# Fourteen Strassen-like pairs in place of thirteen in the down projection of a hybrid decoder layer, with small tiles shared to make room

## The chip, the core and the metric

The kernel runs on one core of a Trainium2 chip. The metric is the device time of one execution in microseconds (us). The engines named below are TensorE (PE, the matrix engine; PEld is its loading of weights), VectorE (DVE), ScalarE (ACT), GpSimd (POOL) and SyncE (SP), whose queue issues nearly all DMA transfers. SBUF is the on-chip memory of 128 partitions from which the engines work, and PSUM holds the matmuls' sums in eight banks.

## The reference

One decoder layer for 256 tokens of width 2048, all in float32:

```
h   = RMSNorm(x);  proj = h @ W_in            (2048 x 6144)
A: 8 heads of stick-breaking attention         (no softmax, strictly causal)
B: 8 heads of rotary, dilated sliding-window attention
mix = concat(head-normalised A, B) @ W_out     (2048 x 2048)
x   = x + RMSNorm(mix)
u   = RMSNorm(x) @ W_up                        (2048 x 11008)
u   = causal depthwise convolution of width 3 over tokens, plus a bias
y   = gelu(gate half of u) * (value half of u) (256 x 5504)
x   = x + RMSNorm(y @ W_down)                  (5504 x 2048)
```

The result has to keep float32 accuracy.

## The kernel before

**Accuracy.** TensorE multiplies in a reduced float32 form. Each weight tile and each activation is therefore split in two: `high` (L86) rounds the tile on ACT into `wh`, `low` (L91) subtracts that from the tile on DVE and leaves the rest in `wl`. Each product is then three matmuls: high by high, activation's low by weight's high, activation's high by weight's low. In the down projection these are lines 597, 598 and 599 (`multiply`). Weights come in half-chunks of 128 x 1024 (512 KB) into five `raw` buffers; `wh` and `wl` have four buffers each.

**Stages.** A list of chunks of 1 MB runs through the value, query and key projections (L729 to L735, with the heads' attention stepped in between), the output projection, a hand-written and pinned passage for the two norms (L754 to L849), and then the 86 chunks of up (43 feature tiles, gate and value half). The chunk loop loads two chunks ahead and splits one ahead. After the loop the down projection runs on its own.

**Who sets the order.** The kernel is written for a framework that plans the order of each engine's instructions from the program order and its own durations, allocates tiles, and adds every wait. `pin` and `keep_in_program_order` bind an instruction to the written order.

**The up stage.** `convolved` (L463) handles one finished chunk. `both` (L125) copies one half of the PSUM sum into a tile `half` on ACT (L128) and adds the other half on DVE into `u` (L130). Then DVE multiplies by the norm's row `r2B` (L468), ACT applies the first tap and the bias into `cv` (L470), and DVE adds the other two taps from `u` (L471, L472). For the gate half ACT applies the gelu (L474). For the value half DVE multiplies gate and value, and stores the result for down: a feature tile that is a "single" goes to `yt` (L480 to L482), one that belongs to a pair goes into the tile `pair` (L487).

**Pairs and singles.** Two feature tiles that form a pair go through a fast 2 x 2 block product: the two k tiles, the two token tiles and the two column blocks of 512 need seven products in place of eight. When a pair's second tile is ready, DVE forms four sums of its blocks (L490 to L493), and ACT and DVE split all seven blocks (L494, L495) into `yp`. Of the 43 feature tiles, 13 pairs take 26 and 17 are singles. The weights' sums are formed in two steps. T13 is formed early: `presum` (L540) loads the two parts during attention and the output projection, adds them (L551) and stores the tile back to memory. Two more sums, T24, are formed in down by L580 and L582 in a part of `room`, the memory of the activations of up. A pair is then four units of work (Rb, Ra, T13 and T24, with 2, 1, 2 and 2 products, L504), a single is one unit of four products (L510).

**The down stage.** It runs twice, for the two halves (`cp`) of the output columns. `_down_plan` (L40) gives the order of pairs and singles: with `cp` 0 two singles first, then the pairs with 11 singles spread among them, then four singles; with `cp` 1 the pairs with 13 singles spread among them, and the last four singles held. `run` (L621) prepares units three ahead (`prepare`, L567: loads, `high`, `low`, T24's sums) and multiplies unit by unit. After the last pair `combine` (L602) adds the shared products with one copy on ACT (L606) and four additions on DVE (L607 to L610). After the first half, `close` (L612) adds each of four banks to the result (L617), takes the sum of squares (L412), and leaves a multiplication by the gain row `gbc` (L619) for later. The held singles go bank by bank, so that each bank can be closed while PE works on the next; the last is split in two halves of 256 columns. The row `gbc` is loaded into `room` and multiplied by -0.5 (L876) just before `down.run()`.

**Small tiles.** `ones` and `diag` serve `along_rows` (L281), which turns a per-token factor into a row by a matmul (L287). It is used by the first norm and, in the passage before up, by the second norm (L436). `phB` is the pool of up and down and takes the space of the attention's pool `apool` once that is closed (L850).

## Time and profile before

| | |
|---|---|
| median of 3 runs | 1117.37 us (1117.27 to 1118.07) |
| profiled execution | 1117.53 us, its span 1115.6 us |
| granted TensorE clock | 0.998 |
| busy: PE, PEld | 1103.6 us, 941.2 us |
| busy: DVE, ACT, POOL | 880.8 us, 658.6 us, 3.3 us |
| DMA moved | 257.79 MB, mean 231 GB/s |

Busy time is the time in which an engine works on instructions. Matmuls overlap, so that PE's busy time says little on its own: the step from one start to the next does. A row of the timeline has the start in us, the length in us, the engine, the line of the kernel, the operation, what it writes and reads, its shape and how many like it are merged; a bracket gives the idle time before it and what ended it. A grouped row has the count after the x, then busy us and the mean ns of one, then the engine's idle time before them. A row of waits gives us in total, how many times, and the longest.

### The profile page before, as it was taken

Reading aid. Unit: us, or ns where it says so; the run is one execution under the profiler, and the core shown is the slowest. Engines: PE = TensorE matmul, PEld = TensorE weight load, DVE = VectorE, ACT = ScalarE, POOL = GpSimd, SP = SyncE. Lnnn points to the kernel's source line nnn. Section 1 sums busy time; section 2 is a strip of 40 time slices with the busy share of each in tenths; the row PEclk is TensorE's granted clock in tenths of the full one; section 3 lists DMA queues with packets and bytes.
Section 4 is the critical chain, followed back from the end, with each engine's and each line's share of the span. In section 5 each row is a group of like instructions: output and inputs, shape, how many; then the busy total and the mean of one; then the engine's idle time right before and its main releaser. Section 6 shows DMA issues by size and latency. Waiting matters only on the chain.

```text
span 1115.6 us, 16292 instructions
## 1 busy us (share of the span) xinstructions
PE 1103.6 (99%) x5855; PEld 941.2 (84%) x5855; DVE 880.8 (79%) x1370; ACT 658.6 (59%) x1038; POOL 3.3 (0%) x10
## 2 busy tenths in 40 slices
PE   9999999999999999999999999999999999999996
PEld 6888888888888888888888888888888888888885
DVE  6577776777776589878888878888878898889887
ACT  6656655655654476655555555555555566666564
POOL 0000000000000000000000000000000000000000
PEclk9999999999999999999999999999999999999999
DMA  9977777878879856555555555555555577767775
GB/s 348 327 259 276 254 249 271 299 256 274 272 259 321 273 199 212 191 188 189 187 190 181 189 187 186 188 187 189 189 188 189 172 251 245 248 218 252 242 242 207
DMA packets 74817, 257.79 MB, mean 231 GB/s; under 512 B 8432, under 2 KB 9328, under 8 KB 73968
## 3 DMA queue, kind: packets, MB, share of 16 engines
q1 hardware_dynamic: 74448, 256.68, 69.0%
q8 instruction: 46, 0.75, 0.3%
q14 instruction: 35, 0.29, 0.1%
q10 hardware_dynamic: 288, 0.07, 0.0%
HBM read 238.89 MB, written 17.83 MB: 230 GB/s over the span
## 4 chain that ended last, share of the span: by engine, by line
PE 98%; DMA 1%; DVE 0%; ACT 0%; issue 0%; SPq 0%; DVEq 0%; ACTq 0%
PE mmu L101 28%; PE mmu L104 14%; PE mmqk L101 11%; PE p L598 7%; PE p L597 7%; PE p L599 6%; PE mmqk L104 5%; PE mmv L147 3%; PE mmo L143 3%; PE mmo L144 3%; PE mmo L147 3%; PE mmv L143 3%; PE mmv L144 3%; PE mmu L110 1%; DMA raw<-in_w_v 1%; PE po L317 0%
## 5 line engine op out<-in xcount | busy, mean ns | idle before, releaser
L88 ACT CAST wh<-raw 128x1024 fp32r<-128x1024 f32 (+1 forms) x413 | 419.5, 1023 | 362.7 <-PE mmu L101 189.6
L93 DVE TENSOR_TENSOR wl<-raw,wh 128x1024 fp32r<-128x1024 f32 (+1 forms) x413 | 487.7, 1187 | 170.8 <-ACT wh L88 167.3
L101 PE MATMUL mmu<-hT,wh 128*128 128x512 f32 x1344 | 340.9, 396 | 0.0
L101 PEld LDWEIGHTS mmu<-hT,wh 128*128 128x128 f32 x1344 | 240.2, 188 | 45.6
L104 PEld LDWEIGHTS mmu<-hT,wl 128*128 128x128 f32 x1344 | 182.9, 189 | 15.2
L104 PE MATMUL mmu<-hT,wl 128*128 128x256 f32 x1344 | 186.4, 281 | 0.0
L101 PE MATMUL mmqk<-hT,wh 128*128 128x512 f32 x512 | 133.0, 401 | 0.0
L101 PEld LDWEIGHTS mmqk<-hT,wh 128*128 128x128 f32 x512 | 92.0, 188 | 17.2
L104 PEld LDWEIGHTS mmqk<-hT,wl 128*128 128x128 f32 x512 | 69.9, 188 | 5.8
L598 PE MATMUL p<-wh,yp 128*128 128x512 f32 x182 | 71.7, 394 | 0.0
L597 PE MATMUL p<-wh,yp 128*128 128x512 f32 x182 | 71.3, 392 | 0.0
L104 PE MATMUL mmqk<-hT,wl 128*128 128x256 f32 x512 | 71.1, 281 | 0.0
L599 PE MATMUL p<-wl,yp 128*128 128x512 f32 x182 | 70.8, 389 | 0.0
L598 PE MATMUL p<-wh,yt 128*128 128x512 f32 (+1 forms) x140 | 54.2, 387 | 0.0
L597 PE MATMUL p<-wh,yt 128*128 128x512 f32 (+1 forms) x140 | 54.0, 385 | 0.0
L599 PE MATMUL p<-wl,yt 128*128 128x512 f32 (+1 forms) x140 | 53.3, 382 | 0.0
L470 ACT ACTIVATE cv<-u,par 128x256 f32<-128x256 f32 x86 | 51.5, 599 | 2.4 <-DVE u L468 2.3
L143 PE MATMUL mmv<-wh,hT 128*128 128x512 f32 x128 | 51.5, 403 | 0.7 <-ACT hT L225 0.6
L144 PE MATMUL mmv<-wh,hT 128*128 128x512 f32 x128 | 50.5, 395 | 0.3 <-DVE hT L248 0.3
L143 PE MATMUL mmo<-wh,mix 128*128 128x512 f32 x128 | 50.4, 394 | 0.0
L88 ACT CAST wh<-room 128x1024 fp32r<-128x1024 f32 x26 | 27.3, 1050 | 38.2 <-PE p L598 37.3
L144 PE MATMUL mmo<-wh,mix 128*128 128x512 f32 x128 | 49.9, 390 | 0.0
(173 smaller groups left out, 1207.2 us busy)
## 6 DMA issues: line engine op xcount, KB each, us to landing
raw<-in_w_up SPq DMA_DIRECT2D x172, 512.0 KB, 4.4
raw<-in_w_qk SPq DMA_DIRECT2D x64, 512.0 KB, 4.9
raw<-in_w_dn SPq DMA_DIRECT2D x60, 512.0 KB, 4.4
raw<-in_w_o SPq DMA_DIRECT2D x32, 512.0 KB, 4.8
raw<-in_w_v SPq DMA_DIRECT2D x31, 512.0 KB, 5.3
t<-in_w_dn SPq DMA_DIRECT2D x26, 512.0 KB, 5.7
t_kept<-t SPq DMA_DIRECT2D x26, 512.0 KB, 3.9
raw<-t_kept SPq DMA_DIRECT2D x26, 512.0 KB, 4.4
```

What stands on the lines that cost most here:

```text
L88: pin(A.copy(wh, raw))
L93: pin(V.tensor_tensor(wl, raw, wh.bitcast(F32), op=ALU.subtract))
L101: T.matmul(ps, wh[:, j * P:(j + 1) * P], h[:, k, :, :], start=(k == 0), stop=False, skip_group_check=True)
L104: T.matmul(ps[:, 0, :], wl[:, j * P:(j + 1) * P], h[:, k, 0, :], start=False, stop=(k == KT - 1), skip_group_check=True)
L110: T.matmul(ps[:, part, :], parts[k // 8][low][:, k % 8 * P:(k % 8 + 1) * P], h[:, k, part, :], skip_group_check=True, **kw)
L143: T.matmul(ps[t], hi[:, k, tc_], ws, start=(first and i == 0 and j == 0), stop=False)
L144: T.matmul(ps[t], lo[:, k, tc_], ws, start=False, stop=False)
L147: T.matmul(ps[t], hi[:, k, tc_], wl[:, j * 512:(j + 1) * 512], start=False, stop=(last and i == len(parts) - 1 and j == n - 1))
L470: A.activation(cv, u, AF.Identity, scale=cw(2), bias=par[:, P_CB + f:P_CB + f + 1])
L597: T.matmul(ps, yh, wh[:, cs], start=key not in self.begun, stop=False)
L598: T.matmul(ps, yl, wh[:, cs], start=False, stop=False)
L599: T.matmul(ps, yh, wl[:, cs], start=False, stop=self.left[key] == 0)
```

## The change

- There are 14 pairs and 15 singles. Pairs are still the tiles 3m and 3m+1.
- The first half of down opens with three singles. The others are spread with the count rounded up, so that a single comes after the first pair rather than later. Without the four at the end it is 8 singles among 14 pairs in the first half and 11 in the second.
- `presum` has 28 sums over 52 steps in place of 26 over every second step. An addition follows its load by two steps (before: three), a store by three (before: four).
- `both` copies into `u` itself and adds in place; `half` goes there. The value half's `cv` lies in the tile `pair`, the gate half's in a tile `gate`.
- `ones` and `diag` are one tile, allocated anew for the second norm under the tag `pair` and filled by GpSimd there.
- The multiplication of `gbc` by -0.5 comes in the middle of the first half of down.

```diff
-NPAIR = 13
+NPAIR = 14
+SUM_STEPS = 52
@@ _down_plan
-    plan = [("one", left.pop(0)) for _ in range(0 if cp else 2)]
+    plan = [("one", left.pop(0)) for _ in range(0 if cp else 3)]
...
-        plan += [("one", left.pop(0)) for _ in range((m + 1) * spread // NPAIR - m * spread // NPAIR)]
+        plan += [("one", left.pop(0)) for _ in range(-(-(m + 1) * spread // NPAIR) + (-m * spread // NPAIR))]
@@ both
-        half = pool.tile([P, S], F32, tag="half", name="half", bufs=1)
-        A.copy(half, ps[:, 1, :])
         u = pool.tile([P, S], F32, tag=name, name=name, bufs=1)
-        V.tensor_tensor(u, ps[:, 0, :], half, op=ALU.add)
+        A.copy(u, ps[:, 1, :])
+        V.tensor_tensor(u, ps[:, 0, :], u, op=ALU.add)
@@ along_rows
-    ones = cpool.tile([P, P], F32, name="ones")
-    G.memset(ones, 1.0)
+    ones = apool.tile([P, 2 * P], F32, name="ones", bufs=1)
+    G.memset(ones[:, 0:P], 1.0)
...
-            dg = small.tile([P, P], F32, tag="diag", name="diag", bufs=1)
+            dg = ones[:, P:2 * P]
             V.tensor_scalar(dg, ident, r[t], None, op0=ALU.mult)
-            T.matmul(ps[:, t * P:(t + 1) * P], ones, dg, start=True, stop=True)
+            T.matmul(ps[:, t * P:(t + 1) * P], ones[:, 0:P], dg, start=True, stop=True)
@@ second_norm
         rs = [sq.newton(*sq.mean(t)) for t in range(2)]
+        ones = phB.tile([P, 2 * P], F32, tag="pair", name="ones", bufs=1, padded_shape=[P, 7 * P])
+        G.memset(ones[:, 0:P], 1.0)
@@ convolved
-        cv = phB.tile([P, S], F32, tag=f"cv{s}", name="cv", bufs=1)
+        m, odd = p // (FT // NPAIR), p % (FT // NPAIR)
+        if s == 0:
+            cv = phB.tile([P, S], F32, tag="gate", name="gate", bufs=1)
+        else:
+            if p in SINGLES or odd == 0:
+                pair[0] = phB.tile([P, 7, P], F32, tag="pair", name="pair", bufs=1)
+            at = 0 if p in SINGLES else 2 * odd
+            cv = pair[0][:, at:at + 2, :].rearrange("p a b -> p (a b)")
...
+            V.tensor_tensor(cv, gate[0], cv, op=ALU.mult)
             if p in SINGLES:
                 n = SINGLES.index(p)
-                V.tensor_tensor(cv, gate[0], cv, op=ALU.mult)
...
-            V.tensor_tensor(y[:, 2 * odd:2 * odd + 2, :], gate[0], cv, op=ALU.mult)
@@ Down.presum
-            pair, odd = divmod(tick, 2)
-            if not odd and 0 <= pair - 2 < len(self.presums):
-                t13, _, kept = self.summed[pair - 2]
+            def due(lag):
+                n, k = len(self.presums), tick - lag
+                return next((p for p in range(n) if SUM_STEPS * p // n == k), None)
+
+            pair = due(3)
+            if pair is not None:
+                t13, _, kept = self.summed[pair]
                 tc.keep_in_program_order(nc.sync.dma_start(kept, t13))
-            if odd and 0 <= pair - 1 < len(self.presums):
-                t13, one, _ = self.summed[pair - 1]
+            pair = due(2)
+            if pair is not None:
+                t13, one, _ = self.summed[pair]
...
-            if not odd and pair < len(self.presums):
+            pair = due(0)
+            if pair is not None:
                 one, two, kept = self.presums[pair]
@@ Down.run
                     self.prepare(u + 1 + self.AHEAD)
+                    if cp == 0 and u == n // 2:
+                        tc.keep_in_program_order(V.tensor_scalar(gbc, gbc, -0.5, None, op0=ALU.mult))
                     self.multiply(u)
@@ layer_kernel
-    V.tensor_scalar(gbc, gbc, -0.5, None, op0=ALU.mult)
```

More of the change, by code (lines that the diff above doesn't have):

```diff
@@ L279, in layer_kernel, with along_rows @@
     rstd1 = cpool.tile([P, 2], F32, name="rstd1")
-    def along_rows(r, name):
+    def along_rows(r, name, ones):
         ps = ps_at.tile([P, S], F32, tag="at", name=name)
         for t in range(2):
-            dg = small.tile([P, P], F32, tag="diag", name="diag", bufs=1)
+            dg = ones[:, P:2 * P]
             V.tensor_scalar(dg, ident, r[t], None, op0=ALU.mult)
-            T.matmul(ps[:, t * P:(t + 1) * P], ones, dg, start=True, stop=True)
+            T.matmul(ps[:, t * P:(t + 1) * P], ones[:, 0:P], dg, start=True, stop=True)
         return ps
@@ L300, in first_norm @@
         V.tensor_copy(rstd1, rstd_of(v0, 2))
-        rps = along_rows((rstd1[:, 0:1], rstd1[:, 1:2]), "rps")
+        rps = along_rows((rstd1[:, 0:1], rstd1[:, 1:2]), "rps", ones)
         V.tensor_scalar(rB[:, 0, :], rps, SCALE, None, op0=ALU.mult)
@@ L438, in second_norm @@
         rs = [sq.newton(*sq.mean(t)) for t in range(2)]
+        ones = phB.tile([P, 2 * P], F32, tag="pair", name="ones", bufs=1, padded_shape=[P, 7 * P])
+        G.memset(ones[:, 0:P], 1.0)
         r2B = cpool.tile([P, S], F32, name="r2B")
-        V.tensor_scalar(r2B, along_rows(rs, "r2ps"), -0.5, None, op0=ALU.mult)
+        V.tensor_scalar(r2B, along_rows(rs, "r2ps", ones), -0.5, None, op0=ALU.mult)
         return r2B
@@ L476, in convolved @@
         else:
-            m, odd = p // (FT // NPAIR), p % (FT // NPAIR)
+            V.tensor_tensor(cv, gate[0], cv, op=ALU.mult)
             if p in SINGLES:
                 n = SINGLES.index(p)
-                V.tensor_tensor(cv, gate[0], cv, op=ALU.mult)
                 A.copy(yt[0][:, n, :], cv)
@@ L483, in convolved @@
                 return
-            if odd == 0:
-                pair[0] = phB.tile([P, 7, P], F32, tag="pair", name="pair", bufs=1)
             y = pair[0]
-            V.tensor_tensor(y[:, 2 * odd:2 * odd + 2, :], gate[0], cv, op=ALU.mult)
             if odd == 1:
```

## The prediction

> **What bounds the kernel now.** The page was read first: its head, the busy times and the chain that ended last.
>
> ```profile
> span 1115.6 us, 16292 instructions
> ...
> PE 1103.6 (99%) x5855; PEld 941.2 (84%) x5855; DVE 880.8 (79%) x1370; ACT 658.6 (59%) x1038; POOL 3.3 (0%) x10
> ...
> PE 98%; DMA 1%; DVE 0%; ACT 0%; issue 0%; SPq 0%; DVEq 0%; ACTq 0%
> ```
>
> TensorE (PE) sets the end nearly everywhere, so an edit pays in two ways only: fewer or shorter matmuls, or PE waiting less. The profiled execution took 1117.53 us, 1.93 more than its span and 0.16 above the median of the runs, 1117.37.
>
> The down projection comes next, since the change alters its matmul count. The timeline of PE there, by start, length and matmul:
>
> ```profile
> 888.38 0.40 PE L597 MATMUL p<-wh,yt 128*128 128x512 f32 x1
> ...
> 897.54 0.40 PE L598 MATMUL p<-wh,yp 128*128 128x512 f32 x1
> 897.94 0.50 PE L599 MATMUL p<-wl,yp 128*128 128x512 f32 x1
> 898.28 0.39 PE L597 MATMUL p<-wh,yp 128*128 128x512 f32 x1
> ...
> 1106.99 0.28 PE L599 MATMUL p<-wl,yt 128*128 128x256 f32 x1
> ```
>
> Forty starts lie between 888.38 and 897.54: 0.229 us each, though each lasts 0.39 (they overlap), so matmuls are priced by that pitch. The steps to 897.94 and 898.28 are 0.40 and 0.34, which is 0.17 and 0.11 too long: PE stood for 0.28 us. 942 full matmuls at 0.229 and 24 of half width at about 0.118 make 218.5 us, and the stage lasts 218.7 or so; it holds no other stall worth naming.
>
> **Fewer matmuls: -1.37 us.** The grouped lines count products (one matmul of L598 each):
>
> ```profile
> L598 PE MATMUL p<-wh,yp 128*128 128x512 f32 x182 | 71.7, 394 | 0.0
> L598 PE MATMUL p<-wh,yt 128*128 128x512 f32 x132 | 52.0, 394 | 0.0
> ```
>
> 182 is 13 pairs x 7 products x 2 column halves. The singles are 17 x 4 x 2 = 136: 132 full and four split into halves. With 14 pairs and 15 singles it is 196 + 120 = 316 products in place of 318: two fewer, of three matmuls each, so 6 x 0.229 = 1.37 us of PE. The end follows only if nobody makes PE wait.
>
> The Trainium skill, "TensorE: Matmul & The Clock Gate", section "Back-to-back issue gap", gives about 131 ns a matmul for a long stream at 512 columns and about 216 for an isolated one. By the first the six would be worth 0.79 us, by the second 1.29; this trace has 229, and that decides.
>
> **More VectorE (DVE) work beside fewer matmuls.** What a pair costs DVE is read where the kernel before already runs two pairs in a row:
>
> ```profile
> 938.98 0.69 DVE L580 TENSOR_TENSOR room<-raw 128x512 f32<-128x512 f32 x1
> ...
> 941.92 1.22 DVE L93 TENSOR_TENSOR wl<-raw,wh 128x1024 fp32r<-128x1024 f32 x1
> 943.20 1.23 DVE L93 TENSOR_TENSOR wl<-room,wh 128x1024 fp32r<-128x1024 f32 x1
> 944.34 2.35 DVE L93 TENSOR_TENSOR wl<-raw,wh 128x1024 fp32r<-128x1024 f32 x2
> 946.61 0.68 DVE L580 TENSOR_TENSOR room<-raw 128x512 f32<-128x512 f32 x1
> ```
> ```profile
> 941.54 0.39 PE L597 MATMUL p<-wh,yp 128*128 128x512 f32 x1
> ...
> 944.06 0.39 PE L599 MATMUL p<-wl,yp 128*128 128x512 f32 x1
> ...
> 945.44 0.39 PE L599 MATMUL p<-wl,yp 128*128 128x512 f32 x1
> ```
>
> From 938.98 to 944.34 DVE makes one pair ready: 5.36 us. Two splits follow in 2.27, so a single costs 1.14. PE needs 21 x 0.229 = 4.81 for a pair and 12 x 0.229 = 2.75 for a single. A pair loses DVE 0.55 of its lead, a single wins 1.61. Before, the pattern was mostly pair, single: 6.50 of DVE in 7.56 of PE. In the first half the change leaves eight singles among 14 pairs, so five times pair, pair, single: 11.86 in 12.37. DVE still fits with 0.5 us to spare. The second half has 11 singles and two such places. Within a double pair the lead must bear about 1.1 us at most; in these rows, in the second of two pairs, the split begun at 941.92 was done at 943.14 and its matmul came at 944.06 (0.92 early), the next was done at 944.43 for 945.44 (1.01 early). Cost taken: 0. If that cover is gone, each further double pair costs what the first one of the kernel before cost, 0.28.
>
> The Trainium skill, "VectorE: DVE Perf Modes", section "The DRAIN you can't avoid", says that the next operation waits until the pipe is empty. Taken strictly, operations would follow at their full durations. Starts 1.14 apart at 1.22 of length, in the rows above, disagree. What it would do here is the second rival.
>
> **The opening: -0.28 us.** The old plan ran single, single, pair, pair, and DVE also scaled the gain row just then:
>
> ```profile
> 893.67 1.22 DVE L876 TENSOR_SCALAR room<-room 128x2048 f32<-128x2048 f32 x1
> ```
>
> The new plan opens single, single, single, pair, single and drops that operation from the place: about 2.75 us more of PE before the first pair, some 1.1 less of DVE, and no double pair. Bounds: 0 to -0.28; taken -0.28. The scaling goes to the 36th of the 71 units of the first half. That is the first unit of the second pair of a double pair, and DVE has by then split four units ahead, so it stands right ahead of the split of the single that follows. The same split of before, begun at 944.34, was done at 945.56; its matmul came 23 x 0.229 after 941.54, at 946.81: 1.25 us early, of which the scaling takes about 1.15. So it just fits, and the single's 1.61 restores the lead. Bounds 0 to 1.1; taken +0.1.
>
> **The end of each half: +0.2 us.** In the last pair of a half the new plan leaves no single behind it, so the four additions that combine the products lose 2.75 us of cover. In the first half four singles follow anyway. In the second half, PE goes straight to the held singles, whose first bank takes one product of each of four; the twelfth matmul wants the low part of the fourth. Before:
>
> ```profile
> 1093.30 0.39 PE L597 MATMUL p<-wh,yt 128*128 128x512 f32 x1
> ...
> 1099.02 0.62 PE L599 MATMUL p<-wl,yt 128*128 128x512 f32 x2
> 1099.47 0.39 PE L597 MATMUL p<-wh,yt 128*128 128x512 f32 x1
> ```
> ```profile
> 1094.44 0.68 DVE L607 TENSOR_TENSOR room<-p,room 128x512 f32<-128x512 f32 x1
> ...
> 1097.50 1.22 DVE L93 TENSOR_TENSOR wl<-raw,wh 128x1024 fp32r<-128x1024 f32 x1
> ...
> 1099.45 0.69 DVE L617 TENSOR_TENSOR room<-p,room 128x512 f32<-128x512 f32 x1
> ```
>
> The last pair ended at 1093.30. That split, begun at 1097.50, was done at 1098.72, just late, and the planned order had put two matmuls of the next bank ahead, so PE lost nothing. The nearest row for the new end is the close of the first half, where four singles follow:
>
> ```profile
> 984.12 0.39 PE L597 MATMUL p<-wh,yt 128*128 128x512 f32 x1
> ```
> ```profile
> 985.26 0.69 DVE L607 TENSOR_TENSOR room<-p,room 128x512 f32<-128x512 f32 x1
> 985.86 1.22 DVE L93 TENSOR_TENSOR wl<-raw,wh 128x1024 fp32r<-128x1024 f32 x1
> 986.99 0.69 DVE L608 TENSOR_TENSOR room<-p,room 128x512 f32<-128x512 f32 x1
> ```
>
> There the fourth single's low part is done 2.96 us after the pair's end; at the new end it is wanted 11 x 0.229 = 2.52 after it, or 2.98 with the same two matmuls put ahead. So PE loses between 0 and 0.44, and if all four additions went ahead of the split, three more at 0.6, up to 2.2. I take 0.2, nearest to the row. The three additions left then push the first closing addition (L617) to about 4.7 us behind the pair's end, in place of 2.9; by the third bank that is made up, as PE needs 2.75 us for each.
>
> **Edits hidden under PE.** In up, ACT now copies straight into `u` and so waits for the last reader of the chunk before, where the separate `half` was free earlier:
>
> ```profile
> 573.47 0.48 DVE L472 SCALAR_TENSOR_TENSOR cv<-u,par,cv 128x254 f32<-128x254 f32 x1
> ...
> 575.00 0.42 DVE L130 TENSOR_TENSOR u<-mmu,half 128x256 f32<-128x256 f32 x1
> ```
> ```profile
> 573.53 0.37 ACT L128 COPY half<-mmu 128x256 f32<-128x256 f32 x1
> ```
>
> The copy would start 0.4 us later, at 573.95, and still end before its reader's 575.00. Behind it on ACT stand the splits, which are ready long before PE wants them, and four banks take the chunks in turn. Cost 0; uncovered, 0.4 on a chunk or 34 us over 86 chunks, of which no row shows a beginning.
>
> The ones of the second norm are now set by GpSimd just before their use, in space that the attention's tiles leave:
>
> ```profile
> L270 POOL MEMSET negones<- 128x128 f32 x1 | 0.2, 204 | 0.3 <-POOLq L944 0.3
> ```
> ```profile
> 416.29 0.62 ACT L412 ACTIVATE jks<-x 128x512 bf16<-128x512 f32 x1
> ```
> ```profile
> 421.36 0.43 PE L287 MATMUL r2ps<-diag,ones 128*128 128x128 f32 x2
> ```
>
> The last work on those tiles ends at 416.91, the fill takes 0.2, the first matmul that reads it starts at 421.36: 4 us of cover, 0.2 without it. One more pair is formed in up: four small operations and one wide split take the place of two singles' splits:
>
> ```profile
> L495 DVE TENSOR_TENSOR yp<-pair,yp 128x896 fp32r<-128x896 f32 x13 | 14.1, 1085 | 0.0
> L551 DVE TENSOR_TENSOR t<-b,t 128x1024 f32<-128x1024 f32 x26 | 31.7, 1220 | 0.0
> ```
> ```profile
> ACT wh L88 <- PE mmqk L101: 65.2, 52, 2.2
> ```
>
> A pre-summed tile (L551) appears twice more: 2.4 us of DVE, two loads and a store each on SP's queue, in the attention stages. The sums run one step earlier after their loads; SP still meets each store one step behind its addition. There ACT waits for buffers that PE holds, not for DMA, so it is all ahead of PE. In up, too, PE is the engine of the chain. Cost 0, at most 2 x 1.2 plus some 2 for the pair.
>
> **The sum.** 1117.53 - 1.37 - 0.28 + 0.1 + 0.2 = 1116.18 for a profiled execution; 0.16 less for the median: 1116.0, 0.12% faster. That is inside 0.2% (2.2 us), about what a measurement of this kernel can tell from no change.
>
> **Rivals.**
> - The tail (chance 0.10). All additions ahead of the fourth split: 2.2 in place of 0.2, 1118.0. For it: they come first in the program's text; against: the planned order of both halves before mixes them.
> - DVE is short in double pairs (0.08). At full durations (three halves at 0.69 and three splits at 1.22) a pair is 5.7 and pair, pair, single 12.7 in 12.37, so 0.3 a time; or 0.28 for each of seven. About 1.5 to 2.0: 1117.7. Against: the second double pair of before ran without a stall.
> - Slower (0.08): loads come late. A double pair fetches six tiles in 9.6 us through five buffers. At the first one of before ACT waited for DMA:
>
> ```profile
> 903.34 0.62 ACT L88 CAST wh<-raw 128x512 fp32r<-128x512 f32 x1 [1.01 <-DMA raw<-in_w_dn]
> 904.62 1.06 ACT L88 CAST wh<-raw 128x1024 fp32r<-128x1024 f32 x1 [0.66 <-DMA raw<-t_kept]
> ```
>
> These 1.67 us, less the 0.92 of lead, at each of seven places make 5.2: 1121.2. It decides once a wait passes the lead. Against: no such wait at the second double pair.
>
> **How the numbers follow.** The forecast has 0.64 and its own range is 1115.4 to 1116.8. The three rivals take 0.26; 0.10 is left to things without a row, such as a new planned order elsewhere, 0.06 of it for a gain beyond 2.2, since the known gains stop at 1.65 and a measurement's scatter must add to them, and 0.04 for a loss. The range 1115.1 to 1118.2 takes in both first rivals and leaves out the third. Faster by over 0.2%: 0.07; within: 0.81; slower: 0.12 (the third rival and the unnamed losses).
>
> **What would show it.** L598 has 196 lines with yp. PE's starts stay 0.229 apart from the first product on; a wider step names the failed part: within double pairs (second or third rival, told apart by whether ACT waits for DMA), or after the last pair (first rival). The forecast is wrong if PE's stage is not 1.2 to 1.7 us shorter, or if waits of PE appear before 888.

## The result, and the profile after

The changed kernel takes 1119.48 us (median of 18 runs, 1118.4 to 1124.04), the kernel before 1117.62 (18 runs, 1117.24 to 1118.24): a ratio of 1.0022 with the interval 1.0016 to 1.0028. It is slower by 0.22%; forecast were 1116.0 us and "within 0.2%". Its profiled execution took 1119.03 us. Of the runs further down, the profiled execution of a_spread ran at a granted clock of 0.556 and took 1829.72 us, so it has no stage and no tail in the table. The head of its page, the busy times, the chain that ended last, and the groups of the pairs' and the singles' first matmuls:

```profile
span 1117.2 us, 16373 instructions
...
PE 1102.8 (99%) x5849; PEld 940.4 (84%) x5849; DVE 889.8 (80%) x1383; ACT 658.3 (59%) x1041; POOL 4.6 (0%) x11
...
PE 95%; DVE 2%; DMA 1%; ACT 1%; issue 0%; SPq 0%; DVEq 0%; ACTq 0%
...
L608 PE MATMUL p<-wh,yp 128*128 128x512 f32 x196 | 77.2, 394 | 0.0
...
L608 PE MATMUL p<-wh,yt 128*128 128x512 f32 (+1 forms) x124 | 48.1, 388 | 0.7 <-DVE u L130 0.7
```

The change does what it says: 5849 matmuls in place of 5855, 196 products of pairs. But PE's share of the chain fell from 98% to 95%, and a line of up (L130) holds up the first matmuls of down. The timeline of PE there, and its last matmul:

```profile
893.76 0.40 PE L610 MATMUL p<-wl,yp 128*128 128x512 f32 x1
894.22 0.47 PE L608 MATMUL p<-wh,yt 128*128 128x512 f32 x1
894.53 0.39 PE L609 MATMUL p<-wh,yt 128*128 128x512 f32 x1
...
896.82 0.40 PE L610 MATMUL p<-wl,yp 128*128 128x512 f32 x1
897.89 0.47 PE L608 MATMUL p<-wh,yt 128*128 128x512 f32 x1 [0.67 <-DVE u L130]
898.20 0.39 PE L609 MATMUL p<-wh,yt 128*128 128x512 f32 x1
...
1106.84 0.28 PE L610 MATMUL p<-wl,yt 128*128 128x256 f32 x1
```

The steps to 894.22 and 897.89 are 0.46 and 1.07, so 0.23 and 0.84 above the pitch of 0.229; with the short losses behind them and one of 0.07 at 891.00 the opening loses 1.30 us, where it lost 0.28 before. Down's first product is at 888.41 (before 888.38). Two lengths carry the comparison from here on: the *stage*, from down's first product to the end of the last matmul, and the *tail*, from there to the end of the span (the page gives the span to 0.1 us, so a tail is good to 0.05).

| | first product | stage | tail | span |
|---|---|---|---|---|
| before | 888.38 | 218.89 | 8.33 | 1115.6 |
| after | 888.41 | 218.71 | 10.08 | 1117.2 |

The stage is 0.18 us shorter: 1.37 saved, 1.30 - 0.28 more lost at the opening, 0.16 in two small steps later. The tail is 1.75 longer. These two make the 1.6 us of the span.

**Where the opening's wait comes from.** The additions that read the chunks' sums out of PSUM, on DVE, of before and then of after; and ACT of after:

```profile
889.18 0.42 DVE L130 TENSOR_TENSOR u<-mmu,half 128x256 f32<-128x256 f32 x1
```
```profile
890.13 0.42 DVE L130 TENSOR_TENSOR u<-mmu,u 128x256 f32<-128x256 f32 x1
...
892.67 0.48 DVE L481 SCALAR_TENSOR_TENSOR pair<-u,par,pair 128x254 f32<-128x254 f32 x1
...
893.65 0.42 DVE L130 TENSOR_TENSOR u<-mmu,u 128x256 f32<-128x256 f32 x1
...
897.32 0.42 DVE L130 TENSOR_TENSOR u<-mmu,u 128x256 f32<-128x256 f32 x1 [0.81 <-ACT u L129]
```
```profile
893.24 0.38 ACT L129 COPY u<-mmu 128x256 f32<-128x256 f32 x1 [1.13 <-DVE pair L481]
...
896.94 0.35 ACT L129 COPY u<-mmu 128x256 f32<-128x256 f32 x1
```

Before, one chunk was still to be read when down began, 0.8 us after its first product. After, there are three, the last 8.9 us after it: the copy into `u` starts 0.09 us after the last reader of the chunk before (892.67 + 0.48 = 893.15), and the banks that the chunks hold are those down wants next. Put against PE, which takes 5.627 us for a chunk, the additions of before start 9 to 11 us behind the end of their chunk at the first three chunks of up and 1.3 to 1.9 from the twelfth on; those of after start some 13 us behind (12.6 to 13.5) from the second chunk to the last but two.

**Where the tail's time comes from.** ACT and then DVE at the end, of before and of after:

```profile
1098.30 1.11 ACT L669 COPY x1p<-x1b 128x512 f32<-128x512 f32 x2 [1.24 <-DMA x1b<-x_kept]
1100.17 0.63 ACT L412 ACTIVATE jks<-room 128x512 bf16<-128x512 f32 x1 [0.77 <-DVE room L617]
```
```profile
1107.30 0.42 DVE L617 TENSOR_TENSOR room<-p,room 128x256 f32<-128x256 f32 x1 [0.22 <-PE p L599]
```
```profile
1100.50 1.11 ACT L682 COPY x1p<-x1b 128x512 f32<-128x512 f32 x2 [3.64 <-DMA x1b<-x_kept]
1101.55 0.63 ACT L412 ACTIVATE jks<-room 128x512 bf16<-128x512 f32 x1
```
```profile
1099.38 0.69 DVE L628 TENSOR_TENSOR room<-p,room 128x512 f32<-128x512 f32 x1
1099.99 0.68 DVE L620 TENSOR_TENSOR room<-p,room 128x512 f32<-128x512 f32 x1
1100.70 0.69 DVE L621 TENSOR_TENSOR room<-p,room 128x512 f32<-128x512 f32 x1
1102.30 0.69 DVE L630 TENSOR_TENSOR room<-room 128x512 f32<-128x512 f32 x1 [0.90 <-ACT jks L412]
...
1108.57 0.42 DVE L628 TENSOR_TENSOR room<-p,room 128x256 f32<-128x256 f32 x1
```

ACT waits 3.64 us for the residual rows `x1b` in place of 1.24, and the squares of the first closed bank (L412), done on DVE's side at 1100.07, start behind those copies at 1101.55. DVE still has additions of the last pair (L620, L621) between the closings. Before, DVE's last closing came 0.03 us after PE's last matmul had ended (1106.99 + 0.28) and waited for it; after, it comes 1.45 after (1106.84 + 0.28), a backlog.

### The profile page after: what moved, and what is told of

The parts are those of the page before. It is cut to its first block, busy times and chain, and to the rows that moved or that the text cites. A ratio compares the mean times of both kernels' runs of the same rounds, so it can differ in the third digit from the quotient of the medians.

```text
span 1117.2 us, 16373 instructions
## 1 busy us (share of the span) xinstructions
PE 1102.8 (99%) x5849; PEld 940.4 (84%) x5849; DVE 889.8 (80%) x1383; ACT 658.3 (59%) x1041; POOL 4.6 (0%) x11
## 4 chain that ended last, share of the span: by engine, by line
PE 95%; DVE 2%; DMA 1%; ACT 1%; issue 0%; SPq 0%; DVEq 0%; ACTq 0%
PE mmu L102 28%; PE mmu L105 14%; PE mmqk L102 11%; PE p L608 6%; PE p L610 6%; PE p L609 6%; PE mmqk L105 5%; PE mmv L147 3%; PE mmo L143 3%; PE mmo L144 3%; PE mmo L147 3%; PE mmv L144 3%; PE mmv L143 3%; PE mmu L111 1%; DMA raw<-in_w_v 1%; DMA x1b<-x_kept 1%
## 5 line engine op out<-in xcount | busy, mean ns | idle before, releaser
L608 PE MATMUL p<-wh,yp 128*128 128x512 f32 x196 | 77.2, 394 | 0.0
L610 PE MATMUL p<-wl,yp 128*128 128x512 f32 x196 | 76.8, 392 | 0.0
L609 PE MATMUL p<-wh,yp 128*128 128x512 f32 x196 | 76.1, 388 | 0.0
L608 PE MATMUL p<-wh,yt 128*128 128x512 f32 (+1 forms) x124 | 48.1, 388 | 0.7 <-DVE u L130 0.7
L610 PE MATMUL p<-wl,yt 128*128 128x512 f32 (+1 forms) x124 | 47.7, 386 | 0.0
L609 PE MATMUL p<-wh,yt 128*128 128x512 f32 (+1 forms) x124 | 47.3, 382 | 0.0
L610 PEld LDWEIGHTS p<-wl,yp 128*128 128x128 f32 x196 | 36.8, 188 | 8.7 <-DVE wl L94 0.2
```

Of the source, the lines that this page charges most:

```text
L608: T.matmul(ps, yh, wh[:, cs], start=key not in self.begun, stop=False)
L609: T.matmul(ps, yl, wh[:, cs], start=False, stop=False)
L610: T.matmul(ps, yh, wl[:, cs], start=False, stop=self.left[key] == 0)
```

## The experiments

Three places were to be told apart. First, the copy into `u` (opening), against a loss from the new plan of pairs and singles. Second, the end of the second half: the residual rows that land late, against the additions of the last pair. Third, which showed itself only once the first was mended: the double pairs (a pair right behind a pair), short of loads or short of VectorE. Ratios are to the kernel before, run beside. Stage and tail are of one profiled execution, whose own time is given with them: it can lie up to 1.7 us off the median, so a difference of a few tenths between two stages says little of the medians.

| run | median us | ratio (interval) | profiled us | stage | tail |
|---|---|---|---|---|---|
| b_inplace | 1118.90 | 1.0012 (1.0003 to 1.0021) | 1119.25 | 220.29 | 8.41 |
| a_half | 1119.37 | 1.0019 (1.0010 to 1.0028) | 1120.23 | 219.38 | 9.85 |
| a_single | 1118.24 | 1.0006 (0.9997 to 1.0014) | 1118.15 | 218.96 | 9.13 |
| a_x1p | 1120.29 | 1.0026 (1.0016 to 1.0036) | 1121.14 | 220.01 | 10.74 |
| a_x1p_act | 1119.27 | 1.0017 (1.0008 to 1.0026) | 1119.16 | 218.90 | 9.65 |
| a_half_single | 1117.88 | 1.0002 (0.9993 to 1.0010) | 1117.35 | 217.97 | 8.66 |
| a_half_t13 | 1122.80 | 1.0050 (1.0037 to 1.0063) | 1122.80 | 223.12 | 8.93 |
| a_best | 1123.98 | 1.0052 (1.0038 to 1.0066) | 1125.12 | 225.44 | 8.60 |
| a_raw6 | 1125.58 | 1.0071 (1.0057 to 1.0085) | 1126.39 | 226.33 | 9.08 |
| a_half_single_raw6 | 1124.81 | 1.0063 (1.0050 to 1.0076) | 1125.21 | 225.69 | 8.63 |
| a_room | 1118.12 | 1.0005 (0.9996 to 1.0014) | 1118.35 | 219.52 | 8.40 |
| a_pool | 1138.74 | 1.0186 (1.0171 to 1.0201) | 1140.39 | 241.00 | 8.64 |
| a_spread | 1116.89 | 0.9988 (0.9978 to 0.9997) | 1829.72 | - | - |
| a_spread_2 | 1116.45 | 0.9990 (0.9981 to 1.0000) | 1116.67 | 217.45 | 8.66 |
| a_spread_x1p | 1118.59 | 1.0004 (0.9995 to 1.0014) | 1118.52 | 218.90 | 8.83 |
| a_spread_act | 1116.62 | 0.9993 (0.9983 to 1.0002) | 1117.15 | 217.34 | 8.98 |

### The copy into u, alone and undone

b_inplace is the kernel before with the copy of the change; a_half is the changed kernel with the tile `half` back.

```diff
 b_inplace (a_half is the reverse, in the changed kernel)
-        half = pool.tile([P, S], F32, tag="half", name="half", bufs=1)
-        A.copy(half, ps[:, 1, :])
...
-        V.tensor_tensor(u, ps[:, 0, :], half, op=ALU.add)
+        A.copy(u, ps[:, 1, :])
+        V.tensor_tensor(u, ps[:, 0, :], u, op=ALU.add)
```

> The kernel before with one edit alone: ACT copies straight into u and DVE adds in place, no separate half. Theory 1 (the copy has to wait for the last reader of u, L472, so a chunk's steps form one closed ring and the lag behind PE that up begins with is never made up): the addition L130 stays some 13 us behind its chunk's end through all of up, as in the changed kernel, in place of 1.5 to 1.8; the first matmuls of down wait for PSUM banks and PE loses 0.8 to 1.5 us there; about 1118.5 to 1119.1. Rival (the opening's stalls come from the fourteenth pair at the end of up and from the new order of units): lag 1.5 to 1.8 us and the time of before, 1117.6 within 0.3.

> The changed kernel with the separate half tile back in up. Theory 1: the lag falls to under 2 us after some ten chunks, the opening of down runs at steps of 0.229 us with at most 0.3 lost, PE ends 1.0 to 1.3 us earlier than in the changed kernel and the time falls by as much, 1119.5 to about 1118.3; the end of down stays late. Rival (fourteenth pair and order of units): stalls of 1.3 us at the opening stay and so does 1119.5.

The copy alone makes the kernel before 1.2 us slower (1118.90 against 1117.67), with the same 13 us of lag through up and the same wait in the opening. PE of b_inplace:

```profile
892.78 0.40 PE L598 MATMUL p<-wl,yp 128*128 128x512 f32 x1
893.70 0.47 PE L596 MATMUL p<-wh,yt 128*128 128x512 f32 x1 [0.52 <-DVE u L129]
```

In a_half the lag is 1.3 to 1.9 us again and the opening has no step above the pitch. So the copy is the cause there, and the plan is not. Yet a_half is no faster than the changed kernel, where 1118.3 was expected: its stage loses 1.9 us in three later places (its profiled execution took 0.86 us more than its median). One of them, on SP's queue, DVE and PE:

```profile
903.67 0.33 SPq L576 DMA_DIRECT2D raw<-t_kept  x1
```
```profile
908.81 0.69 DVE L592 TENSOR_TENSOR room<-raw 128x512 f32<-128x512 f32 x1 [1.55 <-DMA raw<-t_kept]
909.42 2.95 DVE L94 TENSOR_TENSOR wl<-raw,wh 128x1024 fp32r<-128x1024 f32 x3
```
```profile
910.02 0.39 PE L610 MATMUL p<-wh,yt 128*128 128x512 f32 x1
910.69 0.50 PE L611 MATMUL p<-wl,yt 128*128 128x512 f32 x1 [0.28 <-DVE wl L94]
```

T13 of a pair is used 5.1 us after SP issued its load, and DVE stood 1.55 us for it; the split that PE wants stands right behind that addition on DVE. PE loses 0.55 here, in the single ahead of the first double pair, and 0.56 at 917.45, in that double pair, where DVE had stood 1.46 us for the next T13. At the third place the moved scaling comes in as well. DVE and PE:

```profile
941.43 0.69 DVE L592 TENSOR_TENSOR room<-raw 128x512 f32<-128x512 f32 x1 [0.68 <-DMA raw<-t_kept]
...
946.79 1.22 DVE L643 TENSOR_SCALAR room<-room 128x2048 f32<-128x2048 f32 x1
947.93 2.35 DVE L94 TENSOR_TENSOR wl<-raw,wh 128x1024 fp32r<-128x1024 f32 x2
```
```profile
948.29 0.40 PE L610 MATMUL p<-wh,yt 128*128 128x512 f32 x1
949.20 0.50 PE L611 MATMUL p<-wl,yt 128*128 128x512 f32 x1 [0.51 <-DVE wl L94]
```

The moved scaling of the gain row stands ahead of the split that PE wants, and PE loses 0.68 and 0.11 behind it. In the changed kernel the same place loses 0.05, with the scaling in the same order: there the addition L591 ahead of it had not waited for its T13, here it waited 0.68 us. The run a_x1p below shows the same pair of cases without any change in that order.

### The end of the halves

```diff
 a_single
-    spread = len(left) - HELD
+    spread = len(left) - HELD - 1
```
```diff
 a_x1p
+            pinned[0] = True
...
-                A.copy(x1p[i], x1s[1][:, i * 512:(i + 1) * 512])
-            pinned[0] = True
+                pin(A.copy(x1p[i], x1s[1][:, i * 512:(i + 1) * 512]))
```
```diff
 a_x1p_act (the squares of the first two closings, banks 2 and 3, in written order, then the copies)
...
-                A.copy(x1p[i], x1s[1][:, i * 512:(i + 1) * 512])
+                tc.keep_in_program_order(A.copy(x1p[i], x1s[1][:, i * 512:(i + 1) * 512]))
```

> The changed kernel with one single moved behind the last pair in each half (one fewer spread among the pairs). Theory 2 and its rival both expect the end after PE's last matmul at 8.3 to 8.7 us in place of 10.2, as before, about 1117.6, narrow spread. If the end stays at 10.2, neither the late load of x1 nor the uncovered additions is the cause. PE's stalls at the opening (1.3 us) stay by theory 1.

> The changed kernel with the closing additions and squares of the held banks and the two copies of x1 on ACT bound to the written order, so that the copies stand behind the squares of the second bank. Theory 2 (ACT's copies wait for a load of x1 that comes late because one single fewer lies before the held ones, and the squares of the first bank stand behind them): the wait of 3.6 us in front of the copies is passed by the squares, the end after PE's last matmul falls from 10.2 to about 8.5 us, about 1117.8, and the spread of the runs narrows to that of before (1 us). Rival (the four additions of combine, uncovered, hold back DVE): no change, 1119.5.

> The changed kernel with ACT alone reordered at the end: the squares of the first two held banks, then the two copies of x1; VectorE's order is as in the changed kernel. In it the squares of the first bank stood behind copies that waited 3.6 us for DMA, and DVE then stood 0.9 us for those squares. Theory 2a (the late x1 is about 1 us of the end, the uncovered additions the other 0.7): the end after PE's last matmul falls from 10.2 to about 9.2, the time by 1.0. Theory 2b (all of it is x1): to 8.5, by 1.7. Theory 2c (all of it is the additions): 10.2 stays.

One single kept behind the last pair of each half takes 1.24 us off the changed kernel's median, although six and three pairs now stand right behind a pair, in place of five and two. The tail falls to 9.13, not to the 8.3 to 8.7 that was expected, and the opening still loses 1.29. ACT at its end:

```profile
1099.33 1.11 ACT L682 COPY x1p<-x1b 128x512 f32<-128x512 f32 x2 [2.17 <-DMA x1b<-x_kept]
1100.38 0.63 ACT L412 ACTIVATE jks<-room 128x512 bf16<-128x512 f32 x1
```

To take ACT's part alone, a_x1p_act puts the squares ahead of the copies: the tail falls from 10.08 to 9.65 and the median by 0.2, inside the scatter. With DVE's closings bound to the written order too (a_x1p), the additions of the last pair all go ahead of the first closing and the tail grows to 10.74. So ACT's order is the smaller part, 0.4 us of tail; that the rest is the uncovered additions with what follows them is what remains, and was not shown on its own. What the late landing of `x1b` costs was not separated either.

The stage of a_x1p is 1.3 us longer as well, in the first half, which the edit doesn't touch: up to the held singles VectorE and ACT run the same operations in the same order as in the changed kernel, the opening loses the same, and behind it PE loses 1.25 us in place of 0.05, of which 0.79 at the scaling. The addition a few operations ahead of the scaling, of the changed kernel and then of a_x1p:

```profile
940.08 0.69 DVE L591 TENSOR_TENSOR room<-raw 128x512 f32<-128x512 f32 x1
```
```profile
941.54 0.69 DVE L591 TENSOR_TENSOR room<-raw 128x512 f32<-128x512 f32 x1 [0.80 <-DMA raw<-t_kept]
```

So the same order loses 0.05 or 1.25 us in these places, and in the worse execution VectorE waits longer for T13 (4.3 us in down in place of 2.3). What makes T13 come later in one execution than in another stayed open.

### Both mended, and the double pairs

```diff
 a_half_single = a_half + a_single
```

> The changed kernel with the separate half tile and one single moved behind the last pair of each half. Theories 1 and 2 together: no stall at the opening (1.3 us in the changed kernel), the end at 8.5 to 9.3 us behind PE's last matmul; what is left are the stalls within double pairs, 0 to 2 us from run to run. About 1117.3 (1116.5 to 1118.5). If the stalls within double pairs grow as the opening's vanish, as in the run with the half tile alone (1.9 us), it stays at 1118.0 or above.

1117.88: 1.6 us faster than the changed kernel, level with the kernel before. Stage 217.97 and tail 8.66; 0.8 us is lost in and about double pairs still (in an execution 0.53 us faster than the median). The next runs tried to take that away. a_half_t13 is a_half, and a_best is a_half_single, with a pair's T13 loaded second instead of third; a_best also scales the gain row at the end of the first half.

```diff
-   tiles += [..., at + 1024:at + 2048], ..., at + 512:at + 1024], kept[cp, j]]
+   tiles += [..., at + 1024:at + 2048], kept[cp, j], ..., at + 512:at + 1024]]
...
```

> The changed kernel with the half tile back, and in each pair the pre-summed tile T13 loaded as the second tile in place of the third. Theory 3 (within double pairs T13 lands late: its load starts only when the first tile of the pair before is split, 4.5 us before it has to be there): waits for DMA loads of t_kept in down fall from 11 us to under 3, PE's 1.9 us of stalls in the double pairs to under 0.8, the time by 1 to 1.5 against the kernel with the half tile alone (1119.4 to about 1118.2). Rival 3 (VectorE is too slow for double pairs at any landing time): stalls and time stay.

> All repairs together: half tile back, one single behind the last pair of each half, T13 loaded second, the gain row scaled at the last four singles of the first half in place of its middle. If the three theories name all that the change lost, PE steps at 0.229 us through down with at most 0.4 us lost, the end is 8.5 to 9.3 us behind PE's last matmul, and the gain of the six matmuls shows: 1116.0 to 1116.6, the time of before less 1.1 to 1.6. If something else is lost, it stays above 1117.

Both lose much more, 4.7 and 8.0 us of PE: the order of loads matters, and the old order is the better one. By the order of the program T13's buffer is the last of the three to be freed, so that the load that takes this buffer next, and all behind it on SP's queue, would start later; that this is the cause was not shown on its own. More buffers were tried next: a sixth (a_raw6, a_half_single_raw6) and, in the first half, two more in the place of the gain row, which is loaded later (a_room). The two versions with the sixth buffer leave out the fourteenth pair's own result.

```diff
 a_raw6, a_half_single_raw6
...
-                self.load(first + 5)
+                self.load(first + 6)
...
+                if len(self.raws) % 6 == 5:
+                    raw = phB.tile([P, src.shape[-1]], F32, tag="raw6", name="raw", bufs=1, padded_shape=[P, HALF])
```
```diff
 a_room
...
+                k = len(self.raws)
+                if k % 7 > 4 and 7 <= k < self.spare:
+                    raw = room[:, 2, (k % 7 - 5) * HALF:(k % 7 - 5) * HALF + src.shape[-1]]
```

> The changed kernel with a sixth raw buffer for down's weight tiles. Its room comes from the activations of the fourteenth pair, which share those of the thirteenth, so the result of that pair is not computed. Theory 4 (the stalls within double pairs, and the spread of the runs, come from loads that land late because only five tiles are in flight or in use): waits of ACT and DVE for t_kept in down fall from 7 to 11 us to under 3, the spread of 1118.4 to 1124.0 narrows to 1.5 us, the median falls by 0.3 to 1.0. The opening's 1.3 us stay. Rival 4 (VectorE's own time per pair, or something outside of down): spread and median stay at 1119.5.

> The same sixth buffer (again without the fourteenth pair's own result) with the half tile back and a single behind each half's last pair. Theories 1, 2 and 4 together: PE steps at 0.229 us through down with under 0.4 us lost, 1116.3 to 1117.0, spread 1 us, against 1117.9 with five buffers. Rival 4: 1117.9 and a spread of 3 us stay.

> A whole version: half tile back, a single behind each half's last pair, and in the first half of down two more raw buffers in the 8 KB that the gain row takes later; the row is loaded at the end of the first half and scaled at the start of the second. Theory 4: the first half's stalls in double pairs are gone, 1116.3 to 1117.2, below the kernel before by 0.5 to 1.3. Rival 4: 1117.9.

None helps: PE loses 9.1, 7.6 and 2.1 us, and VectorE's waits for T13 grow from 3.2 us in a_half_single to some 14 in the two with the sixth buffer. Why VectorE waits longer with a deeper ring stayed open. The next run was to take VectorE work out of each pair without touching what is loaded: T24's second addition goes to GpSimd.

```diff
 a_pool (a_half_single, and)
-                    V.tensor_tensor(t24[:, 512:], t24[:, 0:512], b21, op=ALU.add)
+                    G.tensor_tensor(t24[:, 512:], t24[:, 0:512], b21, op=ALU.add)
```

> The change with the separate half tile back and one single held behind the last pair of each half (median 1117.88 before), and with the second addition that forms T24 (128x512, 0.69 us on VectorE) moved to GpSimd, so that a pair costs VectorE some 0.6 us less. Theory 'VectorE's rate': with 28 x 0.6 us less of VectorE work in the double pairs PE's steps in the first half close; the down stage loses 0.2 us or less in place of 0.7 and the median falls to about 1117.2. Theory 'loads': the second addition frees Ra's buffer; on a slower engine it frees it later, the load behind it starts later, the waits for DMA in down grow above the 6 us or so of the run it is compared with and PE loses 2 us or more: 1119 or above.

It takes 21 us more than the kernel before, and in its profiled execution PE loses 23.5. GpSimd needs 1.6 to 2.2 us in most cases for what took VectorE 0.69, and the waits for T13 grow. The groups of T24's first addition, with what VectorE waited for ahead of it, of a_half and of a_pool:

```profile
L592 DVE TENSOR_TENSOR room<-raw 128x512 f32<-128x512 f32 x28 | 19.2, 686 | 6.5 <-DMA raw<-t_kept 6.0 <-PE mmu L105 0.5
```
```profile
L592 DVE TENSOR_TENSOR room<-raw 128x512 f32<-128x512 f32 x28 | 19.2, 687 | 15.1 <-DMA raw<-t_kept 14.5 <-PE mmu L105 0.5
```

Neither theory can be read from this run, since VectorE's operations together took no less time. GpSimd's addition, and the splits on VectorE beside it; the same three splits take 2.95 us in a_half (the row at 909.42 above):

```profile
909.51 2.14 POOL L594 TENSOR_TENSOR room<-room,raw 128x512 f32<-128x512 f32 x1 [7.51 <-DVE room L592]
```
```profile
910.42 4.04 DVE L94 TENSOR_TENSOR wl<-raw,wh 128x1024 fp32r<-128x1024 f32 x3
```

Beside 21 of the 28 additions a split takes 1.1 us longer than usual, 23.0 us in all, against 28 x 0.69 = 19.3 us taken off VectorE. The last section comes back to this. For late loads against VectorE's rate the evidence is a_half: ahead of each of its three losses VectorE stood idle for a T13.

### Singles dealt out otherwise

```diff
 a_spread (a_half, and)
...
-    plan = [("one", left.pop(0)) for _ in range(0 if cp else 3)]
-    spread = len(left) - HELD
+    plan = [("one", left.pop(0)) for _ in range(0 if cp else 2)]
+    spread = len(left) - (HELD + 1 if cp else 2)
```

> The change with the separate half tile back and the singles dealt out otherwise: two open the first half, 11 stand between its pairs and two close it; in the second half 10 stand between the pairs and five close it. The first half has three places where a pair follows a pair, the second four. If double pairs are what takes back the gain of the repaired opening (1.9 us lost there in the run with the half tile alone, 0.7 in the run with a single held back), PE's stage loses 0.3 us or less and the end is that of the run with a single held back: 1116.5 to 1117.5. If the losses come from the three loads of every pair, wherever singles stand, they stay at 0.7 to 2: 1118 to 1119.

> The run with the singles dealt out, once more, for a profile of it and a second comparison. If its gain is real, the ratio is again 0.9985 to 0.9995, and PE's down stage holds neither the 1.55 us step at 899.92 of the run that scaled the gain row on GpSimd (there a VectorE operation of 256 columns took 3.31 us while GpSimd's scaling ran) nor more than 0.3 us in double pairs; PE's last matmul then ends 1.2 to 1.7 us earlier than before, counted from the first product. If the gain came from elsewhere, the stage shows the stalls of the other runs and the first product comes earlier.

The first half has two places where a pair follows a pair instead of five, the second half three instead of two (the expectation counts one more in each). Two comparisons agree: 1116.89 against 1117.97, and 1116.45 against 1117.54, both 1.1 us or 0.1% faster than the kernel before (the intervals end at 0.9997 and 1.0000), and their runs lie closer together (1116.16 to 1117.46 in the second) than the changed kernel's. The head of the second one's page, and its group of T24's first addition:

```profile
span 1114.9 us, 16322 instructions
```
```profile
L592 DVE TENSOR_TENSOR room<-raw 128x512 f32<-128x512 f32 x28 | 19.2, 685 | 1.4 <-DMA raw<-t_kept 0.9 <-PE mmu L105 0.5
```

VectorE's waits for T13 fall from 6.0 to 0.9 us, while ACT still waits 5.8 us for it (5.1 in a_half); PE loses 0.2 in the whole stage, all of it in the opening. The stage is 218.89 - 217.45 = 1.44 us shorter than before's: the 1.37 of the smaller count, and a little of the old opening. This is the version that is faster than both. What in the new order does it was not taken apart: beside the smaller number of double pairs in the first half, the scaling now falls where no pair follows a pair, and two singles open and two close the half. Two more edits were tried on it: ACT's order at the end as in a_x1p_act, and the gain row scaled on GpSimd (a_spread_x1p has both, a_spread_act the first alone).

```diff
 a_spread_x1p
-                        tc.keep_in_program_order(V.tensor_scalar(gbc, gbc, -0.5, None, op0=ALU.mult))
+                        tc.keep_in_program_order(G.tensor_scalar(gbc, gbc, -0.5, None, op0=ALU.mult))
```

> The run with the singles dealt out, with two edits more: the squares of the closing banks are ordered on ACT ahead of the copies of x1 into PSUM, and the gain row is scaled on GpSimd in place of VectorE (1.2 us of VectorE gone from the middle of the first half). If the last single's loads and ACT's order still hold 0.2 to 0.6 us at the end and the scaling holds part of the middle, it is 0.3 to 0.8 us faster than the run without: about 1116.4. If both are covered, the two agree within 0.3.

> The run with the singles dealt out, and of the two further edits only ACT's order at the end (squares of the closing banks ahead of the copies of x1), with the gain row scaled on VectorE. If the loss of the run with both edits (1118.59 against 1116.89) came from GpSimd's scaling holding up VectorE at the opening of down, this one has no step above 0.3 us there and agrees with the run without the two edits or is up to 0.4 faster: 1116.4 to 1117.0. If ACT's order was the cause, it is again 1118 or more.

a_spread_act agrees with a_spread_2 (1116.62 against 1116.45), so ACT's order is worth nothing that shows in this plan. a_spread_x1p is slower by some 1.7 us, and the scaling on GpSimd is why (see the last section).

### The changed kernel once more

> The changed kernel once more, for a second look at what differs between its executions (1118.4 to 1124.0). Theory 4: stalls of PE within double pairs differ from the first look's 0.05 us and follow waits for t_kept; stalls at the opening (1.3 us) and the end (10.2 us) are the same. Rival: the difference lies at the start of the kernel, before down's first product at 888.4.

1119.66, span 1117.8, PE's steps at the same places (0.07, 0.24 and 0.84 in the opening), tail 10.47. The opening's loss repeats. The single runs up to 1124.04 were not caught in a profile; a_x1p, with the same order up to the held singles, shows 1.2 us of such a difference. Three versions with five or six double pairs in the first half scatter more (1118.4 to 1124.04, 1119.12 to 1121.51, 1116.36 to 1119.29) than a_spread_2, but a_single, with six, does not (1117.97 to 1119.25).

## Why the prediction was wrong, step by step

- **Fewer matmuls, -1.37: right.** a_spread_2 has all of it in its stage.
- **Edits hidden under PE, "Cost 0; uncovered, 0.4 on a chunk": this step failed.** The copy was priced by the time it starts later on one chunk, and "four banks take the chunks in turn" was taken as cover. What the runs show: the lag that up begins with is not made up any more, 13 us stay on all chunks, PE in up does not feel it, and the bill comes where the banks are wanted by someone else, in down's opening: +1.2 us (b_inplace), gone with the tile back (a_half). The prediction looked for a loss in up ("34 us over 86 chunks, of which no row shows a beginning") and not at the next user of the banks.
- **The opening, -0.28: not got**, for the same reason. With the copy undone it comes (a_half has no loss there).
- **The gain row, +0.1 (0 to 1.1): right.** "It just fits" held in the changed kernel, 0.05 us; where a T13 came 0.7 or 0.8 us late just before, the same place cost 0.79 (a_half, a_x1p).
- **The end, +0.2 (0 to 2.2): this step failed too, 1.75.** The place was right, the cost was not the one that was counted: PE's wait for the fourth split cost 0.14. That 1.75 lies under the upper bound is luck, since that bound was one of PE's waiting. The prediction did not follow ACT and DVE on behind the last pair: with 2.75 us less of matmuls there, the residual rows and the additions come into the closings, and the span ends 1.75 us later while PE itself hardly waits. Of that ACT's order is 0.4 (a_x1p_act); how the rest divides stayed open. "By the third bank that is made up" was wrong: DVE was 1.45 us behind at the last one.
- **More VectorE work in double pairs, 0: right in the profiled execution (0.05 in the first half), in part by luck.** The same order lost 1.25 us in a_x1p, and with the opening mended 0.8 to 1.9 us are lost in and about double pairs. The third rival had the right mechanism, a load that is late where pair follows pair, at well under its price of 5.2, and with VectorE rather than ACT as the engine whose wait PE feels. The second rival, VectorE's rate, is not supported: VectorE stood idle for T13 ahead of the losses in a_half. No run took VectorE's work alone away, so it is not ruled out as a part.
- **The other edits at cost 0** (GpSimd's ones, the earlier sums, the 14th pair's forming) left no trace: down's first product comes at 888.41 and 888.38.

As a sum for the profiled executions: -1.37 + 1.02 + 0.16 + 1.75 = +1.56, against -1.35 forecast. The medians are 1.86 us apart; the profiled execution of the changed kernel was 0.45 faster than its median.

## What to carry to other kernels

An in-place step that saves a tile ties a ring's next element to the last reader of the one before: price it not by the delay of one element but by the lag that is no longer made up, and look for the cost where the ring's buffers change hands. When work is taken from the bounding engine just before a stage's close, follow every other engine through the close: what had that time as cover comes out at the end. And one profile is one execution: the same order of instructions lost 0.05 us in one and 1.25 in another, by whether a load landed in time, so a mended place has to be judged by the medians as well as by its own steps.

## What was not expected of the hardware

GpSimd's scaling of the gain row stopped VectorE. In a_spread_x1p the framework let it run at the opening of down, far ahead of its place in the program; GpSimd, then VectorE, then PE:

```profile
894.04 5.54 POOL L643 TENSOR_SCALAR room<-room 128x2048 f32<-128x2048 f32 x1 [476.12 <-DVE wl L94]
```
```profile
893.93 0.42 DVE L487 TENSOR_TENSOR pair<-gate,pair 128x256 f32<-128x256 f32 x1
894.82 3.31 DVE L491 TENSOR_TENSOR yt<-pair,yt 128x256 fp32r<-128x256 f32 x1 [0.47 <-ACT yt L490]
```
```profile
898.14 0.40 PE L610 MATMUL p<-wh,yp 128*128 128x512 f32 x1
899.92 0.50 PE L611 MATMUL p<-wl,yp 128*128 128x512 f32 x1 [1.39 <-DVE wl L94]
```

An operation of 256 columns that takes 0.42 us took 3.31, and PE lost 1.55 + 0.11 us, where a_spread_act loses 0.10 + 0.11 in the same stretch; the two stages differ by 1.56. GpSimd's operation went on to 899.58 by its row, while VectorE's next ones ran at their usual 0.68 from 898.05, so the hold was 2.9 us and not the operation's full length. In a_pool the hold goes both ways: 21 times a split of VectorE that starts beside GpSimd's addition takes 1.1 us longer (2.3 in place of 1.22, 1.78 in place of 0.68) and ends about one usual length after GpSimd's row does; six times the split runs at its usual length and GpSimd's row takes 2.8 to 4.0 us.

The Trainium skill, "SBUF — State Buffer", section "SBUF: two separate sides", says that VectorE and GpSimd share one pair of ports under an exclusive lock, and that a VectorE operation with two SBUF inputs is blocked by a GpSimd operation that reads SBUF. The row at 894.82 and the 21 splits of a_pool agree in kind, and in a_pool the hold lasts to about the end of GpSimd's row; in a_spread_x1p the release 1.45 us before that row's end does not fit "for the whole instruction", unless the row is too long, as spans on GpSimd are rough.
